# A hybrid decoder block on one core: attention's turns dealt out by the kind of dense output, and a fourth place for split rows

## The chip, the cores and the metric

The kernel runs on one core of a Trainium2 chip. The metric is device time in microseconds for one execution, taken as the median over several runs; less is better. One more execution was recorded by the hardware profiler, and all views in this text come from that one.

## The reference

One layer of a decoder block on x, a sequence of 2048 rows of 1024 numbers, all in float32:

- hn = RMSNorm(x); [u | q | k | v] = hn @ w_in, where each of the four parts is 512 wide.
- Pool mixer: u is cut into four groups of 128 columns. Each group takes a causal running mean over a window (2, 4, 8 and 16 rows), subtracts the row itself, multiplies by a 128 x 128 matrix and by a scale.
- Stick-breaking attention with 8 heads of 64: z = q k / 8, and row t gives to an earlier row s the weight sigmoid(z_ts) times the product of (1 - sigmoid(z_tj)) over all j between s and t. The weights multiply v.
- h = x + concat[RMSNorm(pool), RMSNorm(attention)] @ w_out
- y = RMSNorm(h + relu(RMSNorm(h) @ w_up)^2 @ w_down), with a hidden width of 4096.

## The kernel before, in words

The sequence is cut into four tiles of 512 rows (tile 0 to 3). All rows lie transposed: 128 features across the partitions, 512 rows along the free side. To keep float32 accuracy each operand is split into a high and a low part (`split`, lines 145 and 146: ScalarE copies the high part, VectorE subtracts it from the source), and each product is made of three matmuls, high x high, high x low and low x high.

The front half of the program, which the change touches, computes the input projection and attention. The projection of one tile is cut into 16 **dense outputs** of 128 columns (c = 0 to 3 are the four pool groups, 4 to 7 q, 8 to 11 k, 12 to 15 v). One dense output is 24 matmuls of 512 columns (lines 177 to 179, `products`) into one of two PSUM places (`pd`). What follows depends on the kind. For q and k ScalarE and VectorE split the result (`keep_qk`, tile `qk`) and four DMAs store it. For v ScalarE copies it, TensorE transposes it, and a split of the transposed rows is stored (`keep_v`, tile `vt`). For a pool group (`pool_group`) ScalarE copies it to `u`, VectorE makes c + 1 running sums `s` (line 400), the difference `pl` (line 403) and a split (`pls`, ScalarE the high part, VectorE the low one); then come three matmuls of 512 columns (`pp`, lines 410 to 412: the first and the third need the high part, the second the low one), and ScalarE scales the result to `yb`. So a pool output asks much more of VectorE than the others, most of all c = 3, whose window is 16. The splits `qk`, `vt`, `pls` and `mix` (the normed mixer outputs) share a ring of three places in SBUF, tag `st`.

Attention goes by **turns**. A turn is one head of one tile and one half of its 512 rows (`near_unit`): four matmuls for the logits `pz` (lines 630 and 631), two sigmoids `sh` and `sg` on ScalarE, a mask on GpSimd (line 661), a product scan `pc` on VectorE (line 663), a multiply `sg` (line 672, or 668 for the first rows), and in the next turns four transposes `pta` (line 677) with a split `at`, and six matmuls `po` (line 689) with `v`. Every second turn ends a head with a copy and an add (`ot`, lines 647 and 648). Each head's q, k and v are loaded again by SyncE's queue (lines 623 to 625 and 714 to 717). There are 16 turns to a tile, 64 in all, and they stand in one queue (`todo`), filled by `attend` when their q, k and v are there.

How many turns go with a dense output is set by `state["ratio"]`: half-way through a dense output and after it, `advance` adds half the ratio to an account, and takes turns from the queue while the account is above zero; each turn costs 0.27 (`yield 0.27` in `near`). A ratio of 0.4 so gives about one and a half turns to a dense output. `front(q)` writes the order for the tiles a = 2q and b = 2q + 1: first a's outputs of heads 0 to 3 and the pool groups, then a block in which a and b share the weights of heads 4 to 7, then b's pool groups and heads 0 to 3 (for q = 1 in the other order, pool last). It sets the ratio three times for each q:

```python
RATIO_FRONT = (0.3, 0.4, 0.15, 0.4, 0.4, 0.3)
```

Beside this, `later` holds pieces of the norms (squares, sums and normed chunks `nt`, `h`, `mix`), one or two of which go with each dense output. The program is written in this order, and a scheduler then sets the order of the instructions on each engine, within what the data and the marks of the program allow; a turn may so stand later, though not earlier, than the matmul behind which it was written.

The program before, in what the change touches:

Of the kernel before, what the change touches and what calls it, by code (L numbers as in the profile page):

```python
# [9 lines left out]
F32R = mybir.dt.float32r  # L10
# [5 lines left out]
P = 128  # L16
S = 2048
D = 1024
T = 512
# [3 lines left out]
DH = 64  # L23
# [4 lines left out]
TB = T // P  # L28
# [2 lines left out]
WINDOWS = (2, 4, 8, 16)  # L31
PAD = 15
EPS = 1e-6
RATIO_FRONT = (0.3, 0.4, 0.15, 0.4, 0.4, 0.3)
RATIO_TAIL = 0.6
SR = 3
LB = 4
# [4 lines left out]
POOL, EARLY, FIRST = (0, 1, 2, 3), (4, 8, 12, 5, 9, 13), (4, 8, 5, 9, 12, 13)  # L42
# [3 lines left out]
def hymba_block(ctx: ExitStack, tc: tile.TileContext, xT, gains, w_in, pool_w, w_out, w_up, w_down, out):  # L46
# [239 lines left out]
        return (hpb if j % 2 else hpa).tile([P, 2, T], F32R, tag="h", name="h", align_bytes=256)  # L286

    def make_st():
        return pa.tile([P, 2, T], F32R, tag="st", name="mix", align_bytes=256, bufs=3)


    pw = []
# [14 lines left out]
    def note(emit):  # L307
        prog.append((0, emit, False))

    todo, begun, finished, state = [], {}, set(), {"gran": 0, "tick": 0, "due": 0.0}  # L310


    st = [{} for _ in range(NT)]
# [71 lines left out]
    def pool_group(j, g, ps):  # L385
        w = WINDOWS[g]
        if g == 0:
            st[j]["y"] = pa.tile([P, 4, T], F32, tag="yb", name="yb", bufs=1)
        u = pa.tile([P, PAD + T], F32, tag="u", name="u")
        nc.gpsimd.tensor_copy(u[:, 0:PAD], carry[:, g])  # L390
        if j == 0:
            took = nc.vector.tensor_tensor(u[:, PAD:], ps, st[0]["r"], ALU.mult)
        else:
            took = nc.scalar.activation(u[:, PAD:], ps, AF.Copy)
        nc.gpsimd.tensor_copy(carry[:, g], u[:, T:T + PAD])
        cur, lag = u, 1
        while lag < w:
            nxt = pa.tile([P, PAD + T], F32, tag="s", name="s")
            lo = 2 * lag - 1
            nc.vector.tensor_tensor(nxt[:, lo:], cur[:, lo:], cur[:, lo - lag:PAD + T - lag], ALU.add)  # L400
            cur, lag = nxt, 2 * lag
        pl = pa.tile([P, T], F32, tag="ev", name="pl")
        nc.vector.scalar_tensor_tensor(pl, cur[:, PAD:], 1.0 / w, u[:, PAD:], op0=ALU.mult, op1=ALU.subtract)
        if j == 0:
            nc.vector.tensor_tensor(pl[:, 0:w - 1], cur[:, PAD:PAD + w - 1], recip[:, 0:w - 1], ALU.mult)
            nc.vector.tensor_tensor(pl[:, 0:w - 1], pl[:, 0:w - 1], u[:, PAD:PAD + w - 1], ALU.subtract)
        d = pa.tile([P, 2, T], F32R, tag="st", name="pls", align_bytes=256, bufs=3)
        split((d[:, 0], d[:, 1]), pl)
        pp = psx.tile([P, T], F32, tag="px", name="pp")
        nc.tensor.matmul(pp, pw[0][:, 0, g], d[:, 0], start=True, stop=False)  # L410
        nc.tensor.matmul(pp, pw[0][:, 0, g], d[:, 1], start=False, stop=False)
        nc.tensor.matmul(pp, pw[0][:, 1, g], d[:, 0], start=False, stop=True)
        nc.scalar.activation(st[j]["y"][:, g], pp, AF.Copy, scale=gs[:, g:g + 1])
        return took
# [16 lines left out]
        normed(4, part, g, make_st, lambda: st[j]["rm"], mx[j][at:at + 4])  # L431

    def keep_qk(j, c, dst, ps):
        d = pa.tile([P, 2, T], F32R, tag="st", name="qk", align_bytes=256, bufs=3)
        if j == 0:
            t = pa.tile([P, T], F32, tag="ev", name="qkr")
            nc.vector.tensor_tensor(t, ps, st[0]["r"], ALU.mult)
            ps = t
        took = split((d[:, 0], d[:, 1]), ps)
        for e in range(2):  # L440
            for x in range(2):
                nc.sync.dma_start(dst[2 * c + e][j][x * DH:(x + 1) * DH].bitcast(F32),
                                  d[e * DH:(e + 1) * DH, x].bitcast(F32))
        return took

    def keep_v(j, c, ps):
        vf = pa.tile([P, T], F32, tag="ev", name="vf")
        if j == 0:
            took = nc.vector.tensor_tensor(vf, ps, st[0]["r"], ALU.mult)
        else:  # L450
            took = nc.scalar.activation(vf, ps, AF.Copy)
        pt = psx.tile([P, TB, 2, DH], F32, tag="px", name="ptv")
        for b in range(TB):
            nc.tensor.transpose(pt[:, b], vf[:, b * P:(b + 1) * P], ident)
        vt = pa.tile([P, 2, TB, 2, DH], F32R, tag="st", name="vt", align_bytes=256, bufs=3)
        split((vt[:, :, :, 0], vt[:, :, :, 1]), pt.rearrange("p b e d -> p e b d"))
        for e in range(2):
            nc.sync.dma_start(vs[2 * c + e][j].bitcast(F32),
                              vt[:, e].rearrange("p b x d -> p (b x d)").bitcast(F32))
        return took  # L460
# [47 lines left out]
    def front(q):  # L508


        a, b = 2 * q, 2 * q + 1

        def rate(i):
            note(lambda: state.update(ratio=RATIO_FRONT[3 * q + i]))
        rate(0)
        if q == 0:
            note(start)
            note(norm1_first)
            note(pool_weights)
        else:  # L520
            note(lambda: (load_x(b, bigp), norm1_rms(b), norm1(b), pace(2)))
        for i, c in enumerate((EARLY if q else FIRST) + POOL):
            if q == 0 and i == 2:
                note(lambda: load_x(b, x0p))
            if q == 0 and i == 4:
                note(lambda: (norm1_rms(b), catch_up(len(later)), norm1(b)))
            if q == 0 and i == 8:
                note(lambda: (catch_up(len(later)), to_att(), load_x(b + 1, bigp)))
                attend(a, 0)
                attend(a, 1)  # L530
            in_proj(a, c)
            if q and i in (2, 5):
                attend(a, i // 3)
        note(lambda: (catch_up(len(later)), pool_norm(a)))
        rate(1)
        for h2 in (2, 3):
            note(lambda h2=h2: (norm1_rms(2) if h2 == 2 else None) if q == 0 else attn_norm(0) if h2 == 2 else None)
            for c in range(4 + h2, 16, 4):
                in_proj(a, c)
                in_proj(b, c, True)  # L540
            attend(a, h2)
            attend(b, h2)
        note(lambda: (catch_up(len(later)), (load_acc(0), load_mix(0, KD), attn_norm(1)) if q else norm1(b + 1), pace(1)))
        rate(2)
        for i, c in enumerate(EARLY + POOL if q else POOL + EARLY):
            if q == 0 and i == 4:
                note(lambda: pool_norm(b))
            if q == 0 and i == 6:
                note(lambda: pace(2))
            if q and i == len(EARLY):  # L550
                note(lambda: (catch_up(len(later)), pace(1)))
            in_proj(b, c)
            if i in ((2, 5) if q else (6, 9)):
                attend(b, i // 3 % 2 if q else i // 9)
        note(lambda: (catch_up(len(later)), (pool_norm(b), catch_up(len(later))) if q else None))
# [1109 lines left out]
```

## Time and profile before

| what | value |
|---|---|
| median of 3 runs | 1903.73 us (1903.68 to 1907.18) |
| the profiled execution's own time | 1902.05 us |
| its span, first to last instruction | 1900.3 us |
| TensorE matmuls, busy | 1868.9 us (98%), 8883 instructions |
| VectorE, busy | 1481.2 us (78%) |
| ScalarE, busy | 1025.2 us (54%) |
| GpSimd, busy | 238.5 us (13%) |
| mean granted TensorE clock | 0.995 |

The span leaves out some 1.8 us that lie around it. PE is TensorE's matmuls, DVE VectorE, ACT ScalarE, POOL GpSimd, SPq the queue of SyncE. In rows of the timeline the first number is the start in us from the span's start, the second the duration in us; the bracket at the end is the engine's idle time before the row and what ended it. Matmuls overlap, so the time from one start to the next counts, not the duration. In a table of windows PEclk is the clock that was granted, as a share of full speed.

### The profile page before, as it was taken

The numbers are of one execution on the slowest core, as the hardware profiler recorded it, in microseconds if no ns is written. First come the engines' busy times: TensorE is split into PE (matmuls) and PEld (weight loads), VectorE is DVE, ScalarE is ACT, GpSimd is POOL, SyncE is SP. The second block draws the span as 40 slices with busy tenths as digits, with TensorE's granted clock in tenths as the row PEclk, the third lists the DMA queues.
The fourth block names the chain that finished last, engine by engine and source line by source line (L and its number), as shares of the span: only waits on it lengthen the run. The fifth ranks groups of instructions, "written<-read, shape, count | busy, mean of one in ns | idle before, by whom it ended". The sixth has DMA issues, their size and how long they took to land.

```text
span 1900.3 us, 26640 instructions
## 1 busy us (share of the span) xinstructions
PE 1868.9 (98%) x8883; PEld 1554.3 (82%) x8883; DVE 1481.2 (78%) x2151; ACT 1025.2 (54%) x1616; POOL 238.5 (13%) x463
## 2 busy tenths in 40 slices
PE   9999999999999999999999999999999999999997
PEld 7788788788888888777888888887888888888886
DVE  6887789678866886778799988786666677988774
ACT  6565567455644465554567555554332665656543
POOL 0233234122321050000000000000010010020120
PEclk9999999999999999999999999999999999999998
DMA  7676596699888777787899888889999899999852
GB/s 226 212 255 201 177 313 224 194 322 315 281 310 312 278 252 254 284 303 274 307 358 328 303 308 281 298 284 333 388 313 330 281 317 307 332 294 341 289 206 91
DMA packets 222164, 535.91 MB, mean 282 GB/s; under 512 B 26048, under 2 KB 32192, under 8 KB 218176
## 3 DMA queue, kind: packets, MB, share of 16 engines
q1 hardware_dynamic: 217264, 525.46, 79.4%
q0 software_dynamic: 4608, 8.39, 2.4%
q8 instruction: 72, 1.18, 0.3%
q14 instruction: 76, 0.62, 0.1%
q10 hardware_dynamic: 144, 0.26, 0.0%
HBM read 349.46 MB, written 184.55 MB: 281 GB/s over the span
## 4 chain that ended last, share of the span: by engine, by line
PE 50%; DMA 5%; DVE 2%; issue 1%; ACT 1%; POOL 0%; SPq 0%; DVEq 0%; ACTq 0%
PE pb L1291 14%; PE pY L1118 13%; PE pb L1468 12%; PE pZ L1118 7%; PE pX L1118 3%; DMA ar<-sd 1%; DMA hn<-hs 1%; DMA ar<-sdi 1%; PE pb L1408 1%; DMA td<-t 0%; DMA t<-in_w_down_dram 0%; DMA b<-in_w_down_dram 0%; DMA wr<-in_w_down_dram 0%; DVE ad L146 0%; DVE hw L146 0%
## 5 line engine op out<-in xcount | busy, mean ns | idle before, releaser
L1118 PE MATMUL pY<-sa,hw 128*128 128x512 f32 x1536 | 366.3, 390 | 1.9 <-ACT u L1041 1.9
L1118 PEld LDWEIGHTS pY<-sa,hw 128*128 128x128 f32 x1536 | 287.9, 188 | 63.0 <-ACT u L1041 3.4
L1291 PE MATMUL pb<-ad,wd 128*128 128x512 f32 x1344 | 305.4, 389 | 0.7 <-DVE ad L146 0.7
L177 PE MATMUL pd<-h,hl 128*128 128x512 f32 x752 | 297.9, 396 | 1.5 <-DVE qk L146 1.3
L178 PE MATMUL pd<-h,hl 128*128 128x512 f32 x752 | 297.0, 395 | 0.3 <-DVE h L146 0.3
L179 PE MATMUL pd<-h,hl 128*128 128x512 f32 x752 | 297.3, 395 | 0.0
L1291 PEld LDWEIGHTS pb<-ad,wd 128*128 128x128 f32 x1344 | 252.1, 188 | 53.8 <-DVE ad L146 1.5
L1468 PE MATMUL pb<-ad,wd 128*128 128x512 f32 x1104 | 253.9, 390 | 0.9 <-ACT ad L145 0.9
L1468 PEld LDWEIGHTS pb<-ad,wd 128*128 128x128 f32 x1104 | 206.5, 188 | 44.6 <-ACT ad L145 1.3
L146 DVE TENSOR_TENSOR ad<-ar,ad 128x1024 fp32r<-128x1024 f32 x160 | 194.1, 1221 | 44.1 <-ACT ad L145 43.5
L145 ACT ACTIVATE ad<-ar 128x1024 fp32r<-128x1024 f32 x160 | 168.4, 1054 | 95.7 <-PE pb L1468 31.9
L1118 PE MATMUL pZ<-sa,hw 128*128 128x512 f32 x768 | 186.8, 390 | 1.7 <-DVE a L1061 1.7
L1118 PEld LDWEIGHTS pZ<-sa,hw 128*128 128x128 f32 x768 | 143.9, 188 | 32.7 <-DVE a L1061 3.0
L145 ACT ACTIVATE hl<-raw 128x512 fp32r<-128x512 f32 x168 | 104.1, 629 | 115.6 <-PE pd L179 76.7
L177 PEld LDWEIGHTS pd<-h,hl 128*128 128x128 f32 x752 | 142.2, 189 | 29.0 <-DVE qk L146 1.8
L179 PEld LDWEIGHTS pd<-h,hl 128*128 128x128 f32 x752 | 142.0, 189 | 28.2 <-DVE hl L146 0.5
L178 PEld LDWEIGHTS pd<-h,hl 128*128 128x128 f32 x752 | 142.2, 189 | 27.1 <-DVE h L146 0.7
L146 DVE TENSOR_TENSOR hl<-raw,hl 128x512 fp32r<-128x512 f32 x168 | 115.1, 690 | 46.9 <-ACT hl L145 46.5
L1035 ACT ACTIVATE a<-a 128x512 f32<-128x512 f32 x96 | 60.1, 629 | 89.6 <-DVE a L1077 38.5
L146 DVE TENSOR_TENSOR hw<-rt,hw 128x512 fp32r<-128x512 f32 x128 | 86.5, 686 | 25.2 <-ACT hw L145 25.1
L145 ACT ACTIVATE wd<-wq 128x1024 fp32r<-128x1024 f32 x56 | 59.4, 1060 | 77.1 <-PE pb L1291 68.4
L146 DVE TENSOR_TENSOR wd<-wq,wd 128x1024 fp32r<-128x1024 f32 x56 | 68.5, 1222 | 34.3 <-ACT wd L145 32.8
(218 smaller groups left out, 2737.3 us busy)
## 6 DMA issues: line engine op xcount, KB each, us to landing
ar<-sd SPq DMA_DIRECT2D x96, 512.0 KB, 5.9
ar<-sdi SPq DMA_DIRECT2D x64, 512.0 KB, 5.6
rb<-in_w_up_dram SPq DMA_DIRECT2D x30, 1024.0 KB, 6.2
sd<-a SPq DMA_DIRECT2D x104, 256.0 KB, 5.2
raw<-in_w_in_dram SPq DMA_DIRECT2D x50, 512.0 KB, 4.6
sdi<-hr SPq DMA_DIRECT2D x96, 256.0 KB, 5.4
wr<-in_w_down_dram SPq DMA_DIRECT2D x48, 512.0 KB, 5.7
sd<-s SPq DMA_DIRECT2D x88, 256.0 KB, 4.9
```

The source lines that it names most:

```text
L145: nc.scalar.activation(hi, src, AF.Copy)
L146: return nc.vector.tensor_tensor(lo, src, hi.bitcast(F32), ALU.subtract)
L177: nc.tensor.matmul(ps, hl[:, 0, c], hi, start=(k == 0), stop=False)
L178: nc.tensor.matmul(ps, hl[:, 0, c], lo, start=False, stop=False)
L179: last_mm[0] = nc.tensor.matmul(ps, hl[:, 1, c], hi, start=False, stop=(k == n - 1))
L1035: nc.scalar.activation(t, src, AF.Relu)
L1118: nc.tensor.matmul(t, w[:, wx, c], a[:, ax, c % 2], start=first and c == 0 and x == 0, stop=last and c == G - 1 and x == 2, skip_group_che ...
L1291: nc.tensor.matmul(b, t[:, wx, 2 * (kk % 2) + c, i * P:(i + 1) * P], a[:, ax, c], start=p in ("P1", "P5", "P2") and kk == 0 and c == 0 and ...
L1408: nc.tensor.matmul(b[:, cols], block(t, wx, c, n), a[:, ax, c, cols], start=False, stop=(i == 1 and c == 1 and x == 2), skip_group_check=True)
L1468: nc.tensor.matmul(ps[q, n], block(t, wx, c, n), left_[q][:, ax, c], start=(n_ in ("P1", "P3") and kk == 0 and c == 0 and x == 0), stop=(n ...
```

## The change

The ratio now depends on q, on the stage and, in the first and third stage, on whether the output is a pool group. The second number of a pair is that of the pool outputs:

```diff
-RATIO_FRONT = (0.3, 0.4, 0.15, 0.4, 0.4, 0.3)
+PACE = (((0.3, 0.3), 0.4, (0.25, 0.1)), ((0.25, 0.1), 0.4, (0.4, 0.25)))
...
-        return pa.tile([P, 2, T], F32R, tag="st", name="mix", align_bytes=256, bufs=3)
+        return pa.tile([P, 2, T], F32R, tag="st", name="mix", align_bytes=256, bufs=4)
...
-        def rate(i):
-            note(lambda: state.update(ratio=RATIO_FRONT[3 * q + i]))
-        rate(0)
+        def rate(r):
+            note(lambda: state.update(ratio=r))
...
         for i, c in enumerate((EARLY if q else FIRST) + POOL):
+            rate(PACE[q][0][c in POOL])
...
-        rate(1)
+        rate(PACE[q][1])
...
-        rate(2)
         for i, c in enumerate(EARLY + POOL if q else POOL + EARLY):
+            rate(PACE[q][2][c in POOL])
```

The tiles `pls`, `qk` and `vt` get `bufs=4` in the same way as `mix`. So the first stage of q = 0 (tile 0) and both shared blocks keep their ratios. Tile 1's pool outputs go from 0.15 to 0.1 and its other outputs from 0.15 to 0.25; tile 2's from 0.4 to 0.25, its pool outputs to 0.1; tile 3's from 0.3 to 0.4, its pool outputs to 0.25. What a turn computes, and the order of the turns among themselves, stay as they were.

Where the turns go is seen in the order of the instructions. On VectorE, the last pool output of tile 2 (c = 3) before the change: its sums `s` lead to `pl_4176`, `pc`, `sg`, `at` and `ot` are of turns, `ss` is of a norm, `hl` are weights. Ahead of these rows, behind the first sum `s_4168<-u_4164`, stand one more multiply `sg`, one more scan `pc` and one `ss`.

```order
L648 TENSOR_TENSOR ot_4127<-ot_4127,po_4029 64x512
L400 TENSOR_TENSOR s_4170<-s_4168 128x524
L146 TENSOR_TENSOR pls_4082<-pl_4080,pls_4082 128x512
L672 TENSOR_TENSOR sg_4288<-sg_4288,pc_4281 128x2x255
L146 TENSOR_TENSOR at_4214<-pta_4209,at_4214 128x512
L400 TENSOR_TENSOR s_4172<-s_4170 128x520
L146 TENSOR_TENSOR hl_4416<-raw_4106,hl_4416 128x512
L663 SCALAR_TENSOR_TENSOR pc_4347<-sh_4352,later_keys_106 128x512
L400 TENSOR_TENSOR s_4174<-s_4172 128x512
L672 TENSOR_TENSOR sg_4354<-sg_4354,pc_4347 128x2x255
L146 TENSOR_TENSOR at_4277<-pta_4272,at_4277 128x512
L403 SCALAR_TENSOR_TENSOR pl_4176<-s_4174,u_4164 128x512
```

The same place after the change, from the first sum on; `pl_3971` is the same difference.

```order
L400 TENSOR_TENSOR s_3963<-u_3959 128x526
L146 TENSOR_TENSOR at_3998<-pta_3993,at_3998 128x512
L663 SCALAR_TENSOR_TENSOR pc_4002<-sh_4007,later_keys_106 128x512
L400 TENSOR_TENSOR s_3965<-s_3963 128x524
L146 TENSOR_TENSOR pls_3908<-pl_3906,pls_3908 128x512
L189 TENSOR_TENSOR ss_4055<-ss_4055,sq_4057 128x512
L672 TENSOR_TENSOR sg_4009<-sg_4009,pc_4002 128x2x255
L400 TENSOR_TENSOR s_3967<-s_3965 128x520
L400 TENSOR_TENSOR s_3969<-s_3967 128x512
L403 SCALAR_TENSOR_TENSOR pl_3971<-s_3969,u_3959 128x512
```

Between the first sum and `pl` stood 14 rows with two scans; now stand 8 rows with one, and over all four pool outputs of the tile three scans are left of seven.

On TensorE, the three pool matmuls `pp` of that output before the change stand behind the `po` matmuls of two turns, at the end of a dense output (`pd_4424` is the next).

```order
L689 MATMUL po_4331<-at_4277,vw_4197 64x128
L689 MATMUL po_4331<-at_4343,vw_4197 128x256
L689 MATMUL po_4331<-at_4343,vw_4197 128x128
L689 MATMUL po_4331<-at_4343,vw_4197 64x128
L689 MATMUL po_4331<-at_4343,vw_4197 64x256
L689 MATMUL po_4331<-at_4343,vw_4197 128x128
L689 MATMUL po_4331<-at_4343,vw_4197 64x128
L410 MATMUL pp_4181<-pls_4178,pw_656 128x512
L411 MATMUL pp_4181<-pls_4178,pw_656 128x512
L412 MATMUL pp_4181<-pls_4178,pw_656 128x512
L177 MATMUL pd_4424<-h_2455,hl_4103 128x512
```

After the change the same three (`pp_3976`) stand among the last matmuls of the dense output `pd_4091`.

```order
L178 MATMUL pd_4091<-h_3983,hl_3926 128x512
L410 MATMUL pp_3976<-pls_3973,pw_656 128x512
L179 MATMUL pd_4091<-h_3983,hl_3926 128x512
L677 MATMUL pta_4111<-ident_98,sg_4085 128x128 x4
L630 MATMUL pz_4200<-kw_4136,qa_4131 128x256
L411 MATMUL pp_3976<-pls_3973,pw_656 128x512
L412 MATMUL pp_3976<-pls_3973,pw_656 128x512
```

The matmuls of the turns around them have gone to the dense outputs behind; the place itself, about two dense outputs behind the one that they belong to, is the same.

On VectorE, the last pool output of tile 1 before the change, the end of its chain to the split `pls_2649`:

```order
L663 SCALAR_TENSOR_TENSOR pc_2777<-sh_2782,later_keys_106 128x512
L648 TENSOR_TENSOR ot_2766<-ot_2766,po_2662 64x512
L400 TENSOR_TENSOR s_2645<-s_2643 128x512
L672 TENSOR_TENSOR sg_2784<-sg_2784,pc_2777 128x2x255
L740 TENSOR_SCALAR zero_2912<-left0_137 128x16
L146 TENSOR_TENSOR at_2773<-pta_2769,at_2773 128x384
L146 TENSOR_TENSOR hl_2822<-raw_2745,hl_2822 128x512
L403 SCALAR_TENSOR_TENSOR pl_2647<-s_2645,u_2635 128x512
L741 TENSOR_REDUCE zall_141<-zero_2912 128x1
L146 TENSOR_TENSOR pls_2649<-pl_2647,pls_2649 128x512
```

And after the change, the same end:

```order
L400 TENSOR_TENSOR s_2645<-s_2643 128x512
L146 TENSOR_TENSOR hl_2822<-raw_2745,hl_2822 128x512
L663 SCALAR_TENSOR_TENSOR pc_2806<-sh_2811,later_keys_106 128x512
L403 SCALAR_TENSOR_TENSOR pl_2647<-s_2645,u_2635 128x512
L648 TENSOR_TENSOR ot_2795<-ot_2795,po_2712 64x512
L672 TENSOR_TENSOR sg_2813<-sg_2813,pc_2806 128x2x255
L146 TENSOR_TENSOR at_2802<-pta_2798,at_2802 128x384
L740 TENSOR_SCALAR zero_2891<-left0_137 128x16
L146 TENSOR_TENSOR pls_2649<-pl_2647,pls_2649 128x512
```

Here the scan of the third turn stands still ahead of `pl`; `ot`, `sg` and `at` have moved from ahead of it to between `pl` and `pls`.

More of the change, by code (lines that the diff above doesn't have):

```diff
@@ L406, in pool_group @@
             nc.vector.tensor_tensor(pl[:, 0:w - 1], pl[:, 0:w - 1], u[:, PAD:PAD + w - 1], ALU.subtract)
-        d = pa.tile([P, 2, T], F32R, tag="st", name="pls", align_bytes=256, bufs=3)
+        d = pa.tile([P, 2, T], F32R, tag="st", name="pls", align_bytes=256, bufs=4)
         split((d[:, 0], d[:, 1]), pl)
@@ L433, in keep_qk @@
     def keep_qk(j, c, dst, ps):
-        d = pa.tile([P, 2, T], F32R, tag="st", name="qk", align_bytes=256, bufs=3)
+        d = pa.tile([P, 2, T], F32R, tag="st", name="qk", align_bytes=256, bufs=4)
         if j == 0:
@@ L454, in keep_v @@
             nc.tensor.transpose(pt[:, b], vf[:, b * P:(b + 1) * P], ident)
-        vt = pa.tile([P, 2, TB, 2, DH], F32R, tag="st", name="vt", align_bytes=256, bufs=3)
+        vt = pa.tile([P, 2, TB, 2, DH], F32R, tag="st", name="vt", align_bytes=256, bufs=4)
         split((vt[:, :, :, 0], vt[:, :, :, 1]), pt.rearrange("p b e d -> p e b d"))
```

## The prediction

> **What bounds the kernel now.** I read the page first. TensorE is busy nearly the whole span:
>
> ```profile
> span 1900.3 us, 26640 instructions
> PE 1868.9 (98%) x8883; PEld 1554.3 (82%) x8883; DVE 1481.2 (78%) x2151; ACT 1025.2 (54%) x1616; POOL 238.5 (13%) x463
> ```
>
> The change removes no matmul, so all it can win is what is missing there: gaps on TensorE and stretches in which its clock is not granted in full. Then I looked for those in the front half, with a table of windows:
>
> ```profile
> 200.00:210.00 10.00, 6.36 (x38) 5.11 (x36) 9.62 (x19) 4.24 (x8) 4.84 (x3) 1.00 0.69 224
> 210.00:220.00 10.00, 9.43 (x34) 7.43 (x35) 5.79 (x10) 5.37 (x11) 0.00 (x0) 0.83 0.61 150
> 330.00:340.00 10.00, 7.83 (x48) 6.26 (x47) 10.00 (x16) 6.12 (x11) 6.46 (x4) 1.00 0.25 87
> 340.00:350.00 10.00, 9.34 (x38) 7.73 (x39) 8.29 (x13) 4.97 (x9) 0.79 (x3) 0.66 0.65 176
> ```
>
> Columns behind the length: PE, PEld, DVE, ACT and POOL busy, then PEclk. At two places TensorE loses time while VectorE (third) is full, 9.62 and 10.00 of 10 us, and after each the clock is down, to 0.83 and 0.66. The timeline of TensorE shows what waits there:
>
> ```profile
> 210.35 0.50 PE L410 MATMUL pp<-pls,pw 128*128 128x512 f32 x1 [3.98 <-ACT pls L145]
> 211.07 0.79 PE L411 MATMUL pp<-pls,pw 128*128 128x512 f32 x1 [0.22 <-DVE pls L146]
> ...
> 212.09 0.63 PE L177 MATMUL pd<-h,hl 128*128 128x512 f32 x1
> 212.52 0.63 PE L178 MATMUL pd<-h,hl 128*128 128x512 f32 x1
> ...
> 334.54 0.49 PE L411 MATMUL pp<-pls,pw 128*128 128x512 f32 x1 [0.30 <-DVE pls L146]
> ...
> 339.87 0.66 PE L677 MATMUL pta<-ident,sg 128*128 128x128 f32 x4 [1.87 <-DVE at L146]
> 341.19 2.18 PE L689 MATMUL po<-at,vw 128*128 128x256 f32 x12 [0.67 <-DVE ot L648]
> ```
>
> Both stand in the last pool outputs of a tile: stall 1 (tile 1) waits for `pls`, stall 2 (tile 2) for the splits of the turns that pile up there. Stall 1 costs 3.98 + 0.22 = 4.2 us of gaps and (1 - 0.83) x 10 = 1.7 us of clock, 5.9 in all. Stall 2 costs 0.30 + 1.87 + 0.67 = 2.84 us of gaps and (1 - 0.66) x 10 = 3.4 us of clock, 6.2 in all. No other gap behind 112 us in the front reaches 1 us.
>
> **Tile 2, where turns are taken out.** VectorE's rows of the three marks of that place, the first sum of c = 0, the first sum of c = 3 and its `pl`:
>
> ```profile
> 298.89 0.70 DVE L400 TENSOR_TENSOR s<-u 128x526 f32<-128x526 f32 x1
> ...
> 329.66 0.69 DVE L400 TENSOR_TENSOR s<-u 128x526 f32<-128x526 f32 x1
> ...
> 339.74 0.67 DVE L403 SCALAR_TENSOR_TENSOR pl<-s,u 128x512 f32<-128x512 f32 x1
> ```
>
> The prices of single steps come from the same engine at stall 1, from one start to the next, where it ran without a gap; the last rows give the way from `pl` to TensorE, with ScalarE's row between:
>
> ```profile
> 184.47 0.71 DVE L400 TENSOR_TENSOR s<-u 128x526 f32<-128x526 f32 x1 [0.21 <-ACT u L394]
> ...
> 204.72 1.22 DVE L663 TENSOR_TENSOR_SCAN pc<-sh,later_keys 128x512 f32<-128x512 f32 x1
> 205.86 0.65 DVE L648 TENSOR_TENSOR ot<-ot,po 64x512 f32<-64x512 f32 x1
> 206.44 0.67 DVE L400 TENSOR_TENSOR s<-s 128x512 f32<-128x512 f32 x1
> 207.04 0.67 DVE L672 TENSOR_TENSOR sg<-sg,pc 128x510 f32<-128x510 f32 x1
> ...
> 207.88 0.55 DVE L146 TENSOR_TENSOR at<-pta,at 128x384 fp32r<-128x384 f32 x1
> 208.35 0.68 DVE L146 TENSOR_TENSOR hl<-raw,hl 128x512 fp32r<-128x512 f32 x1
> 208.95 0.68 DVE L403 SCALAR_TENSOR_TENSOR pl<-s,u 128x512 f32<-128x512 f32 x1
> ...
> 210.33 0.69 DVE L146 TENSOR_TENSOR pls<-pl,pls 128x512 fp32r<-128x512 f32 x1 [0.62 <-ACT pls L145]
> ```
>
> ```profile
> 209.66 0.63 ACT L145 ACTIVATE pls<-pl 128x512 fp32r<-128x512 f32 x1 [2.63 <-DVE pl L403]
> ```
>
> So a scan takes 205.86 - 204.72 = 1.14 us, a step of 512 columns 207.04 - 206.44 = 0.60, one of 384 columns 0.47, `ot` 0.58. From the start of `pl` to that of the first `pp` go 210.35 - 208.95 = 1.4 us, and the second `pp` follows 211.07 - 210.33 = 0.74 behind the start of VectorE's `pls`. The method can be tested: before the change 14 rows, two of them scans, stand between the sum at 329.66 and `pl`. That makes 13 x 0.60 + 2 x 1.14 = 10.1 us, and the trace has 339.74 - 329.66 = 10.08.
>
> After the change 8 rows with one scan stand there: 8 x 0.60 + 1.14 = 5.9 us. VectorE was also late when it came to that sum: from the first sum of c = 0 it took 329.66 - 298.89 = 30.8 us. In the new order the way between the same marks holds 31 steps, one of them a scan and five of them `nt` (0.67, an estimate from its busy time), which makes 20.3 us. TensorE needs 18.5 us for its own work between the two outputs (an estimate from matmuls at the spacings below). So VectorE comes to that sum 1.8 us late, and `pl` starts some 0.75 + 1.8 + 5.9 = 8.5 us behind the end of the dense output (0.75 is an estimate for ScalarE's copy `u` of 0.6 us and the hand-over), `pp` could start 1.4 us later, at 9.9 us. TensorE's own way to that place, by its order, is 53 matmuls of 512 columns and 32 small ones, at these spacings:
>
> ```profile
> 242.21 0.39 PE L178 MATMUL pd<-h,hl 128*128 128x512 f32 x1
> 242.44 0.39 PE L179 MATMUL pd<-h,hl 128*128 128x512 f32 x1
> 242.66 0.65 PE L689 MATMUL po<-at,vw 128*128 128x256 f32 x6
> 243.14 0.62 PE L677 MATMUL pta<-ident,sg 128*128 128x128 f32 x4
> ```
>
> 53 x 0.227 + 32 x 0.1 = 15.2 us (242.66 - 242.44 gives 0.22; 0.48 / 6 = 0.08 for a `po`, and 0.1 taken as a mean). There are 5 us in hand, so stall 2 goes: -6.2 us. If VectorE came 5 us later than summed, the stall would come back.
>
> **Tile 1, where the order keeps the turns.** The ratio there falls from 0.15 to 0.1, but the order on VectorE, which was never idle from 184.47 (the sum of c = 2) to `pl`, holds in between one scan more (1.14) for one `at` (0.47), one `ot` (0.58) and the small `zero` (0.1, an estimate) less; the other steps are the same. That is a difference of 0.0 us, and `pl` starts where it did, at about 208.95. Behind it `ot`, `sg`, `at` and `zero` now come ahead of `pls`, 0.58 + 0.60 + 0.47 + 0.1 = 1.75 us, so the low half is ready at 208.95 + 0.6 + 1.75 + 0.74 = 212.0 and not at 211.07. TensorE comes to the place with the same matmuls behind it. Stall 1 stays, and grows by 0 to 1 us, nearer to the upper end, as `pls` is a fixed count of steps behind `pl`: I take +0.8. Bounds for the place as a whole: 2 us less if `pl` comes early, 2 us more if the scan ahead of it waits, as its logits now stand just six rows ahead of `pp` on TensorE.
>
> **Where the turns go.** By the ratios 11 turns went with the 12 outputs that tiles 2 and 3 share, and 17 will; tile 3's pool outputs get 4 for 5. That stage stands here (and the wait that is nearest to its danger, TensorE waiting for a PSUM place until VectorE has split `qk`):
>
> ```profile
> 357.00:425.00 68.00, 68.00 (x389) 58.52 (x388) 46.40 (x66) 37.15 (x69) 14.54 (x42) 1.00 0.87 293
> ```
>
> ```profile
> PE pd L177 <- DVE qk L146: 1.3, 2, 0.8
> ```
>
> A turn costs VectorE 1.14 + 0.60 + 0.60 + 0.58 / 2 = 2.6 us; six are 16 us, and this window has 21.6 us idle. The turn brings its 14 matmuls along (some 1.4 us at 0.1), so the window also grows, by the 8 us that tile 2's own stage loses: no change in the sum. GpSimd (mask and a small copy) has 13% to do, and the loads of a head go on SyncE's queue in the same order with the same turns; no row of TensorE is released by a DMA. I cost it at nothing, within 1 us to either side. If the cover is gone, a dense output waits as at those two rows: 0.8 us each without the clock, some 6 with it.
>
> **The ring of four.** It takes away waits on ScalarE:
>
> ```profile
> ACT mix L145 <- DMA vs<-vt: 5.9, 2, 3.7
> ...
> ACT mix L145 <- DMA mx<-mix: 2.9, 1, 2.9
> ```
>
> These 8.8 us are hidden, since ScalarE is busy 54% and TensorE had no gap at those places. I cost it at nothing (0 to -1 us).
>
> **A rule on the clock.** After stall 1 matmuls start 212.52 - 212.09 = 0.43 us apart, about twice 0.227, and after stall 2, whose longest gap is 1.87 us, the window has 0.66. The Trainium skill, "TensorE: Matmul & The Clock Gate", section "What's actually happening", says that the clock goes to half after an idle window of about 3.4 us. The half agrees with the rows; for the gap of stall 2 the trace does not, since 1.87 and 0.67 us were enough. By the rule alone the slow stretch there would have another cause and could remain, and the sum would be less; I go by the rows.
>
> **Sum.** -6.2 + 0.8 = -5.4 us. The profiled execution took 1902.05 us, so 1896.7; the median of the runs stands 1.7 us above it, and on it the forecast is 1898.3. What can be told from no change in this kernel is about 0.2%, 3.8 us.
>
> **The rivals.**
> - Both stalls go: VectorE's `pl` in tile 1 comes over 3.4 us sooner than summed, for instance because ring waits had held it. For it: ScalarE's idle of 2.63 us ahead of `pls`. Against it: that wait ended with VectorE's `pl`. -6.2 - 5.9 = -12.1, 1891.6. Chance 0.08.
> - The slow stretch of stall 2 stays though its gaps go, as other gaps under 2 us bring it about: -2.84 + 0.8 = -2.0, 1901.7. Chance 0.08.
> - One new stall of the size of stall 2 in the stage that now has 17 turns: -5.4 + 6.2 = +0.8, 1904.5, no change. Chance 0.15. For it: the wait at `qk`; against it: 21.6 us of idle time.
> - Slower: VectorE falls behind twice in that shared stage, so that the split of `qk` comes later than the 5.4 us (24 x 0.227) that the other PSUM place covers, each time with the slow clock behind it: -5.4 + 2 x 6.2 = +7.0, 1910.7. It decides from two turns' work (5.2 us) piled up at one dense output. Chance 0.12.
> - That the change does not do what it says holds for tile 1, and is in the sum; for tile 2 the order shows that it does.
>
> **How the numbers follow.** The forecast, stall 2 gone and stall 1 left, has 0.57, and its own range is 1894.5 to 1901 (2 us less or more for stall 1, 1 us each for the shared stage and the ring); 0.04 of it lie within 3.8 us of 1903.7. Faster is 0.53 + 0.08 = 0.61, no change 0.04 + 0.08 + 0.15 = 0.27, slower 0.12. The range leaves out the first and the fourth rival (0.20): 1894 to 1905.
>
> **What would show it.** Right: no gap over 0.5 us at `pp` of tile 2 and PEclk 1.00 there; the gap at `pp` of tile 1 still near 4 us with the clock down behind it; no gap over 1 us in the shared stage of tiles 2 and 3. Wrong: the gap of tile 1 under 1 us, or a new row of TensorE that waits over 1 us for `qk`, `at` or `pls` and a window behind it with a clock under 0.9.

## The result, and the profile after

The changed kernel is slower: 1915.58 us (median of 5 runs, 1912.4 to 1917.46) against 1905.84 us of the kernel before in the same set; the ratio is 1.0062, with a 95% interval of 1.0046 to 1.0077. The forecast was 1898.3, faster. The profiled execution took 1916.48 us, 14.4 us more than that of the kernel before, where the medians are 9.7 us apart; what is counted below is counted in the two profiled ones. The head of its page:

```profile
span 1914.8 us, 26666 instructions
...
PE 1871.9 (98%) x8883; PEld 1558.2 (81%) x8883; DVE 1484.2 (78%) x2151; ACT 1027.1 (54%) x1616; POOL 233.8 (12%) x463
```

The span is 14.5 us longer, and the shares of the engines are what they were: they say nothing. The same table of windows as in the prediction (length; PE, PEld, DVE, ACT and POOL busy; PEclk; DMA share; GB/s):

```profile
200.00:210.00 10.00, 6.06 (x34) 4.66 (x32) 9.97 (x18) 5.94 (x11) 2.86 (x4) 0.99 0.54 185
210.00:220.00 10.00, 9.45 (x33) 7.64 (x34) 5.60 (x10) 3.06 (x6) 0.00 (x0) 0.67 0.57 152
250.00:260.00 10.00, 6.70 (x38) 5.43 (x36) 5.15 (x9) 5.01 (x10) 0.00 (x0) 1.00 0.99 336
260.00:270.00 10.00, 8.38 (x32) 7.00 (x33) 7.39 (x12) 5.04 (x10) 1.26 (x2) 0.66 0.64 201
310.00:360.00 50.00, 50.00 (x281) 42.59 (x281) 44.23 (x69) 29.53 (x54) 20.02 (x33) 1.00 0.72 226
...
357.00:425.00 68.00, 68.00 (x409) 59.10 (x408) 54.79 (x77) 42.87 (x79) 16.31 (x39) 1.00 0.89 293
...
550.00:560.00 10.00, 6.04 (x34) 4.98 (x33) 3.57 (x6) 2.72 (x6) 0.00 (x0) 0.89 1.03 407
560.00:570.00 10.00, 6.29 (x19) 5.33 (x20) 6.90 (x11) 6.13 (x11) 3.50 (x8) 0.50 1.03 393
```

Stall 2 is gone (310 to 360: PE 50.00 of 50, clock 1.00). Stall 1 is there. Two stretches are new, around 260 and around 560 us, and in both VectorE and ScalarE are far from full (2.7 to 7.4 us of 10 busy): this is not an engine that has too much to do. What TensorE waits for there, in its timeline:

```profile
208.86 0.50 PE L410 MATMUL pp<-pls,pw 128*128 128x512 f32 x1 [3.31 <-ACT pls L145]
...
210.55 0.80 PE L411 MATMUL pp<-pls,pw 128*128 128x512 f32 x1 [1.19 <-DVE pls L146]
...
261.62 0.80 PE L177 MATMUL pd<-h,hl 128*128 128x512 f32 x1 [4.92 <-DVE qk L146]
...
563.71 1.86 PE L205 MATMUL pm<-inv,ss 128*128 128x1 f32 x8 [7.67 <-DVE ss L189]
```

The third is **stall 3**: a dense output of tile 2, just behind the end of tile 1, finds no PSUM place, since `qk` has not been split. The last is **stall 4**: in the output projection, which follows the front, the mean `pm` for the norm of tile 2's attention output waits for the sum of squares `ss`. Counted as gap + (1 - clock) x busy time of the windows behind it, stall 1 costs 4.50 + 0.33 x 9.45 = 7.6 us (5.8 before, counted so), stall 3 costs 4.92 + 0.34 x 8.38 = 7.8 (a gap of 0.76 before), stall 4 costs 7.67 + 0.11 x 6.04 + 0.50 x 6.29 = 11.5, and stall 2 nothing (6.0 before). That makes 1.8 + 7.0 + 11.5 - 6.0 = 14.3 of the 14.5 us. That it comes so near is in part chance: TensorE's first matmul of the hidden layers (line 1118), behind all four places, starts 11.5 us later than before (700.7 against 689.2 us), so the count is some 3 us too high, and another 3 us are lost behind that point, where TensorE waits 4.4 us for `a` in place of 1.7.

**How stall 3 comes about.** ScalarE's timeline at that place, and further down the row behind which stall 4 begins:

```profile
248.03 1.66 ACT L145 ACTIVATE mix<-nt 128x512 fp32r<-128x512 f32 x3
...
257.90 0.63 ACT L145 ACTIVATE mix<-nt 128x512 fp32r<-128x512 f32 x1 [4.17 <-DMA vs<-vt]
258.44 0.58 ACT L145 ACTIVATE at<-pta 128x512 fp32r<-128x512 f32 x1
258.92 0.59 ACT L636 ACTIVATE sh<-pz 128x512 f32<-128x512 f32 x1
259.39 0.60 ACT L638 ACTIVATE sg<-pz 128x512 f32<-128x512 f32 x1
259.87 0.61 ACT L145 ACTIVATE qk<-pd 128x512 fp32r<-128x512 f32 x1
...
559.89 0.63 ACT L185 ACTIVATE ss<-ol 128x512 f32<-128x512 f32 x1 [2.58 <-DMA ol<-os]
```

`vt` and three `mix` fill the ring of four. The fourth `mix` needs the place of `vt`, and gets it only when the store `vs<-vt` has landed. ScalarE works in order, so the split of `qk` stands behind that wait, with three rows between, and TensorE behind the split.

**How stall 4 comes about.** SyncE's queue (a row's second number is the time over which its DMAs were issued; `mx` and `os` are where the rows `mix` and the attention output lie in the chip's main memory, and `h<-mx` loads the former again for the output projection):

```profile
250.13 0.85 SPq L458 DMA_DIRECT2D vs<-vt  x2
...
543.78 1.44 SPq L561 DMA_DIRECT2D h<-mx  x2
...
545.86 0.99 SPq L561 DMA_DIRECT2D h<-mx  x2
546.94 0.39 SPq L280 DMA_DIRECT2D mx<-mix  x1
...
553.73 0.33 SPq L159 DMA_DIRECT2D raw<-in_w_out_dram  x1
554.99 0.88 SPq L810 DMA_DIRECT2D ol<-os  x2
```

The load `ol` (tile 2's attention output) waits for the store of tile 3's last `mix`: the program makes it wait for that store, in every kernel here. The store, issued at 546.94, takes 8.0 us to land, and `ol` is issued at 554.99. Before, SyncE's rows, then ScalarE's at the two hand-overs, then TensorE's:

```profile
245.75 0.32 SPq L458 DMA_DIRECT2D vs<-vt  x1
...
540.22 0.32 SPq L280 DMA_DIRECT2D mx<-mix  x1
...
544.88 0.88 SPq L810 DMA_DIRECT2D ol<-os  x2
```

```profile
251.33 0.63 ACT L145 ACTIVATE mix<-nt 128x512 fp32r<-128x512 f32 x1 [2.25 <-DMA vs<-vt]
...
549.98 0.64 ACT L185 ACTIVATE ss<-ol 128x512 f32<-128x512 f32 x1 [0.32 <-DMA ol<-os]
```

```profile
256.07 0.50 PE L177 MATMUL pd<-h,hl 128*128 128x512 f32 x1 [0.76 <-DVE qk L146]
...
555.37 0.95 PE L205 MATMUL pm<-inv,ss 128*128 128x1 f32 x8
```

So both waits stood in the kernel before, and were all but covered: from the start of `ss` to `pm` the chain takes 563.71 - 559.89 = 3.8 us where TensorE waits for it, and before it had 555.37 - 549.98 = 5.4 us. There were 1.6 us in hand. Two things used them up. The order brought the store nearer to `pm`: from its issue to the moment at which `pm` wants to start (its start less its wait, 563.71 - 7.67 = 556.04) there are 556.04 - 546.94 = 9.1 us, before 555.37 - 540.22 = 15.2 us, so 6.1 us less. And the store took 8.0 us to land in place of 4.7, 3.3 us more. Together 9.4 us, less the 1.6 in hand, make 7.8; the wait is 7.67.

### The profile page after: what moved, and what is told of

Its sections match the earlier page's. It is cut to its first block, busy times and chain, and to the rows that moved or that the text cites. A ratio compares the mean times of both kernels' runs of the same rounds, so it can differ in the third digit from the quotient of the medians.

```text
span 1914.8 us, 26666 instructions
## 1 busy us (share of the span) xinstructions
PE 1871.9 (98%) x8883; PEld 1558.2 (81%) x8883; DVE 1484.2 (78%) x2151; ACT 1027.1 (54%) x1616; POOL 233.8 (12%) x463
## 4 chain that ended last, share of the span: by engine, by line
PE 51%; DMA 3%; DVE 2%; issue 1%; ACT 1%; POOL 0%; SPq 0%; DVEq 0%; ACTq 0%
PE pb L1291 16%; PE pY L1118 13%; PE pb L1468 12%; PE pZ L1118 7%; PE pX L1118 3%; DMA hn<-hs 1%; DMA ar<-sd 1%; PE pb L1408 1%; DMA td<-t 0%; DMA t<-in_w_down_dram 0%; DMA b<-in_w_down_dram 0%; DVE hw L146 0%; DVE a L1077 0%; DMA su<-hs 0%; DVE a L1073 0%
```

## The experiments

Ratios are to the kernel before, run on the same chip in the same set (its medians, one for each set: 1901.96, 1903.75, 1903.4 and 1902.43 us). The table sums the runs up: how tile 1, 2 and 3 get their turns ("old" as before, "new" as changed), the places of the ring, and the two waits of TensorE in us, with any other single wait of 2 us or more that the kernel before does not have.

| run | tiles 1, 2, 3 | places | stall 3 | stall 4 | other | ratio, 95% interval |
|---|---|---|---|---|---|---|
| before | old, old, old | 3 | 0.8 | 0 | | 1 |
| after | new, new, new | 4 | 4.9 | 7.7 | | 1.0062 (1.0046 to 1.0077) |
| e1_pace_ring3 | new, new, new | 3 | 5.8 | 0 | `pr` for `yrlast` 4.0 | 1.0035 (1.0023 to 1.0048) |
| e2_ring_only | old, old, old | 4 | 0 | 1.7 | | 1.0014 (1.0001 to 1.0027) |
| e3_tile3_old | new, new, old | 4 | 3.9 | 4.4 | `pY` for `u` 2.2 | 1.0044 (1.003 to 1.0058) |
| e4_tile2_ring3 | old, new, old | 3 | 1.7 | 2.2 | | 1.0011 (1.0001 to 1.002) |
| f1_tile1_old | old, new, new | 4 | 0.5 | 0 | | 0.9957 (0.9944 to 0.9969) |
| f2_tile1_old_ring3 | old, new, new | 3 | 0.9 | 0 | `pY` for `u` 2.0 | 0.9986 (0.997 to 1.0002) |
| g1_vs_on_act | as after | 4 | 3.1 | 8.5 | | 1.0035 (1.0023 to 1.0046) |
| g2_ol_on_act | as after | 4 | 2.7 | 14.3 | `pY` for `u` 2.2, `pd` for `acc` 2.1 | 1.0071 (1.0048 to 1.0093) |
| h1_pool_01 | (0.15, 0.1), new, new | 4 | 1.9 | 0 | | 0.9983 (0.997 to 0.9996) |
| h2_qkv_025 | (0.25, 0.15), new, new | 4 | 0 | 1.6 | | 0.9989 (0.9974 to 1.0004) |
| k3_root_later | as after | 4 | 3.1 | 5.5 | | 1.0043 (1.0029 to 1.0057) |
| e5_tile2_ring4 | old, new, old | 4 | 0 | 0 | `pr` for `yrlast` 4.4 | 0.9988 (0.9976 to 1.0) |
| k4_root_earlier | as after | 4 | 3.1 | 11.7 | | 1.0064 (1.0046 to 1.0083) |

**First four: the ring or the dealing?** The parts of the change, taken apart:

```diff
e1_pace_ring3:   bufs=4 -> bufs=3 in the four tiles of the ring, PACE as changed
e2_ring_only:    RATIO_FRONT as before, bufs=4
e3_tile3_old:    PACE's last pair (0.4, 0.25) -> (0.3, 0.3)
e4_tile2_ring3:  tile 1 (0.15, 0.15), tile 2 (0.25, 0.1), tile 3 (0.3, 0.3), bufs=3
```

> The turns dealt out as in the changed kernel, the ring for split rows left at three places. Theory R (the ring is the fault: with four places the scheduler sets a mix whose place only the slow store of vt gives back ahead of work that TensorE needs): the wait of pd for qk at tile 2's first outputs, 4.92 us in the changed kernel, is under 1.5 us; the wait of pm for ss in the tail, 7.67 us, is under 2 us; stall 2 stays away and stall 1 stays; time 3 to 6 us under the kernel before. Theory T (the dealing of the turns is the fault, the ring does nothing): both new waits stand as in the changed kernel, time 8 to 12 us over the kernel before.

> The turns as in the kernel before, the ring with four places. Theory R: stall 2 stays (a loss of about 6 us as before), the wait of pd for qk at tile 2's first outputs is 4 to 5 us, and there may be a wait of 5 us or more of pm for ss; time 6 to 15 us over the kernel before. Theory T: no new wait over 1.5 us, time within 2 us of the kernel before.

> The changed kernel with tile 3's turns at the old ratio, the ring with four places. Theory R: both new waits stand (4 to 5 us of pd for qk at tile 2's first outputs, 5 us or more of pm for ss), time within 3 us of the changed kernel. Theory T, in the form that tile 3's dealing makes the later wait: the wait of pm for ss is under 2 us and the time is 9 to 13 us under the changed kernel's, the wait of pd for qk stands.

> Only tile 2's turns are dealt out anew, tiles 1 and 3 at the old ratios, three places. Theory R: stall 2 gone, stall 1 as before (about 4 us of gap), no new wait over 1.5 us, time 5 to 7 us under the kernel before. Theory T, in the form that tile 2's dealing is the fault: the wait of pd for qk at tile 2's first outputs is 4 to 5 us, time within 3 us of the kernel before.

Theory R fell at once. With three places stall 3 is there all the same (5.75 us), with four places and the old turns it is not. TensorE's timeline of e1_pace_ring3, with a third wait, that for a root that GpSimd works out, and SyncE's rows for stall 4:

```profile
262.24 0.80 PE L177 MATMUL pd<-h,hl 128*128 128x512 f32 x1 [5.75 <-DVE qk L146]
...
709.58 1.61 PE L231 MATMUL pr<-identr,yrlast 128*128 128x128 f32 x6 [3.97 <-POOL yrlast L834]
```

```profile
539.96 0.53 SPq L280 DMA_DIRECT2D mx<-mix  x1
...
544.20 0.88 SPq L810 DMA_DIRECT2D ol<-os  x2
```

Stall 3 so goes with the dealing. Stall 4 does not stand here, so theory T, which wanted both, fell too. With four places it does, in three sizes in this group (1.7, 4.4 and 7.7 us), but e4_tile2_ring3 has one of 2.2 us with three places: the ring alone does not make it. e3_tile3_old, with tile 3's old turns, kept both waits, stall 4 at 4.4 us, which is neither the 5 us or more of theory R nor the under 2 us of theory T. Stall 2 is gone wherever tile 2 has the new turns, and stands where it has not (e2_ring_only: `pta` for `at` 1.9 us). Neither theory foresaw e4_tile2_ring3: stall 2 gone, and the time still 0.1% over the kernel before; part of what was won at stall 2 shows as longer waits at other hand-overs (2.2 us for `ss`, 1.7 for `qk`, 1.3 more than before for `u` in the hidden layers); where the rest went was not found.

**Next four: one cause or two, and what holds the store and the load up.**

```diff
f1_tile1_old:        PACE's first new pair (0.25, 0.1) -> (0.15, 0.15), bufs=4
f2_tile1_old_ring3:  the same, bufs=3
g1_vs_on_act:        -nc.sync.dma_start(vs[2 * c + e][j]...
                     +(nc.scalar if j == 1 and c == 1 else nc.sync).dma_start(vs[2 * c + e][j]...
g2_ol_on_act:        -nc.sync.dma_start(ol[i], ...
                     +(nc.scalar if j == 2 else nc.sync).dma_start(ol[i], ...
```

> The changed kernel with tile 1's turns at the old ratios (0.15 for all its outputs); tiles 2 and 3 dealt out anew, four places. Theory D (each new wait has its own cause: the earlier one tile 1's dealing whatever the ring, the later one the ring of four, made longer by tile 3's dealing): pd's wait for qk at tile 2's first outputs is under 2 us, stall 1 is back at 4.0 us, the wait of pm for ss stays at 5 us or more; time 5 to 9 us under the changed kernel. Theory C (one cause: the delay made at tile 1 is carried on and brings the later wait): both waits under 2 us, time at or under the kernel before.

> As the run with tile 1's old ratios, with three places. Theory D: stall 2 gone, stall 1 at 4.0 us, neither new wait (each under 2 us); what is left over 1.5 us is small, time 3 to 6 us under the kernel before. Theory S (whatever is dealt out anew, the static order puts some other hand-over too late, as it did in the tail of two runs so far): a new wait of 1.5 us or more somewhere behind 400 us, time within 3 us of the kernel before or over it.

> The changed kernel; the two stores of vt of tile 1's last v output are issued by ScalarE in place of SyncE, on its own DMA queue; the order is otherwise the same, row for row. Theory Q (the store is late because it stands behind a dozen loads of q, k and v on SyncE's queue): it lands 2 to 3 us sooner, the fourth mix waits under 2 us (4.2 now), pd's wait for qk falls from 4.92 to 1 to 3 us and its slow clock with it, time 3 to 7 us under the changed kernel. Theory B (the DMA engines are full, whoever issues): it lands as late, the wait stays over 4 us, time within 3 us of the changed kernel.

> The changed kernel; the two loads ol of tile 2's attention output are issued by ScalarE in place of SyncE, so that they don't stand behind raw there. Theory D (the wait of pm for ss comes from these loads standing behind two weight loads in SyncE's queue): ol is issued before 550 us, the wait of pm for ss (7.67 us) falls under 3 us, time 5 to 10 us under the changed kernel. Rival (pm has been put too early on TensorE's order, and the load only looks late because all of it is): the wait stays over 5 us, time within 3 us of the changed kernel.

f1_tile1_old is the run that tells most: one pair of numbers taken back, and both new stalls are gone. Theory C had that right, theory D, which wanted stall 4 to stay, did not. The time is 1896.16 us against 1903.75, and this is a version that beats both kernels. TensorE's timeline, three windows of the table, and SyncE's rows for stall 4:

```profile
208.72 0.50 PE L410 MATMUL pp<-pls,pw 128*128 128x512 f32 x1 [3.98 <-ACT pls L145]
...
253.31 0.50 PE L177 MATMUL pd<-h,hl 128*128 128x512 f32 x1 [0.52 <-DVE qk L146]
```

```profile
250.00:260.00 10.00, 9.48 (x52) 7.93 (x52) 8.73 (x14) 7.79 (x15) 3.74 (x2) 1.00 0.76 238
...
310.00:360.00 50.00, 50.00 (x294) 43.15 (x293) 43.22 (x64) 31.30 (x58) 16.23 (x33) 1.00 0.86 278
...
550.00:560.00 10.00, 10.00 (x53) 8.54 (x52) 3.79 (x7) 3.16 (x6) 6.61 (x25) 1.00 0.85 298
```

```profile
530.49 0.32 SPq L280 DMA_DIRECT2D mx<-mix  x1
...
533.63 1.43 SPq L810 DMA_DIRECT2D ol<-os  x2
```

f2_tile1_old_ring3 has neither stall, and still comes out near no change, as theory S said: its largest new wait is one of 2.0 us for `u` in the hidden layers.

g1_vs_on_act is inconclusive. Its order is the changed kernel's, but for the two stores. Here are ScalarE's row and TensorE's of it, and then ScalarE's and TensorE's of k3_root_later (below), which leaves this place alone:

```profile
255.41 0.63 ACT L145 ACTIVATE mix<-nt 128x512 fp32r<-128x512 f32 x1 [1.84 <-DMA vs<-vt]
```

```profile
259.13 0.79 PE L177 MATMUL pd<-h,hl 128*128 128x512 f32 x1 [3.06 <-DVE qk L146]
```

```profile
255.54 0.63 ACT L145 ACTIVATE mix<-nt 128x512 fp32r<-128x512 f32 x1 [2.30 <-DMA vs<-vt]
```

```profile
259.26 0.50 PE L177 MATMUL pd<-h,hl 128*128 128x512 f32 x1 [3.06 <-DVE qk L146]
...
564.22 1.86 PE L205 MATMUL pm<-inv,ss 128*128 128x1 f32 x8 [5.51 <-DVE ss L189]
```

The wait of 3.06 us is at the edge of what theory Q expected (1 to 3 us), but a kernel that leaves the stores with SyncE has the same. From issue to the `mix` that waits for it the store took 7.8 us in the changed kernel, 5.2 in e3_tile3_old, 6.2 in g2_ol_on_act, 6.3 in k3_root_later, 6.4 in k4_root_earlier, and 5.5 when ScalarE issued it: no better than the spread. The Trainium skill, "DMA: Bandwidth & Descriptors", section "Issuing engines are not separate DMA queues", says that DMAs of all engines end up on the same 16 DMA engines, and that another issuer saves issue time alone; this run agrees.

The spread serves for something else. In these six kernels, which share the order at this place, the row of TensorE starts 3.72 or 3.73 us behind the start of that `mix`, whether the `mix` came at 253.92 or at 257.90. So it is this wait that TensorE waits out, in each of them.

g2_ol_on_act missed, and no theory had it: the wait grew to 14.3 us. ScalarE issued the loads at 550.98, still 9.2 us behind the store of the last `mix`, and waited for the second of them until 562.93. Why they are so late was seen in the last run.

**Last five.**

```diff
h1_pool_01:       tile 1 (0.15, 0.1)
h2_qkv_025:       tile 1 (0.25, 0.15)
k3_root_later:    -if c == (2 if j == 0 else 4) and j + 2 < NT:
                  +if c == (3 if j == 0 else 4) and j + 2 < NT:
e5_tile2_ring4:   tile 1 (0.15, 0.15), tile 2 (0.25, 0.1), tile 3 (0.3, 0.3), bufs=4
k4_root_earlier:  +if c == (1 if j == 0 else 4) and j + 2 < NT:
```

> The changed kernel with tile 1's q, k and v outputs at the old 0.15 and its pool outputs at the new 0.1. Theory Q (the earlier new wait comes from the 0.25, which puts turns of tile 1, and the loads of their heads, ahead of the last store of vt): pd's wait for qk at tile 2's first outputs is under 2 us, time 4 to 9 us under the changed kernel. Rival P (the 0.1 is the fault: the turns kept out of the pool outputs come later, beside the pool norm): the wait is 4 us or more.

> The changed kernel with tile 1's q, k and v outputs at the new 0.25 and its pool outputs at the old 0.15. Theory Q: pd's wait for qk is 4 to 6 us, time within 4 us of the changed kernel. Rival P: the wait is under 2 us, time 4 to 9 us under the changed kernel.

Neither number alone makes stall 3 (1.9 and 0 us). Rival P fell by the first run, theory Q, which laid it on the 0.25, by the second: it takes both. What the seven kernels with both have in common is the lead of the store. From its issue to the moment at which TensorE wants to start (its start less its wait) there are 5.0 to 7.2 us (the changed kernel 256.70 - 250.13 = 6.6); where the other kernels show it, 8.5 to 9.6 (before 255.31 - 245.75 = 9.6, f1_tile1_old 252.79 - 244.23 = 8.6, h1_pool_01 8.6). In these kernels the store takes 5 to 8 us and the way from `mix` to TensorE 3 to 5, so under some 9 us TensorE waits. But the lead is not all. SyncE's row and TensorE's of h2_qkv_025:

```profile
248.49 0.79 SPq L458 DMA_DIRECT2D vs<-vt  x2
```

```profile
255.84 0.39 PE L177 MATMUL pd<-h,hl 128*128 128x512 f32 x1
```

Its store has a lead of 7.4 us, about that of the seven, and the same row of TensorE did not wait, since the two stores landed in 2.3 and 2.6 us. By the landing times in the traces, one earlier load of SyncE's was still under way when they were issued, in the changed kernel six. (The count alone does not tell it: in h1_pool_01 there were three, and the store took 6.8 us.) So stall 3 takes a store that is both late and slow; what makes it slow was not tried alone. h2_qkv_025 has no wait for `pls` at stall 1's place either (its longest gap there is 1.2 us), and yet it is only 0.1% under the kernel before: TensorE starts its hidden layers 3.3 us earlier (685.9 against 689.2 us), and the profiled span ends 1.9 us later. What it loses behind that point was not followed up.

> The changed kernel; the root of tile 2's attention norm is taken up one output later (at the fourth output of the projection of tile 0 in place of the third). The loads ol keep their place on SyncE, behind the same rows; pm, which waits for them through ss, stands 21 rows of 0.227 us, 4.8 us, later on TensorE. Theory L (the later new wait is the lead that the order leaves between these loads and pm, as the loads come late): the wait of pm for ss falls by 4.8 us, from 7.67 to 2 to 4 us, and the loss there from 11.9 to 3 to 6 us; time 5 to 9 us under the changed kernel. Rival (loads and pm move together, since VectorE, not the load, is late): the wait stays over 6 us.

Half of it: the wait fell by 2.2 us, not by 4.8, to 5.5, as the store took 9.1 us to land and not 8.0, and from the landing of the second load to `pm` went 4.1 us and not 2.2. The ratio is 0.2% under the changed kernel's, with intervals that overlap, where 5 to 9 us had been expected.

> Only tile 2's turns dealt out anew, four places. If tile 3's dealing does nothing of its own: like the run with tile 1's old ratios, 6 to 9 us under the kernel before. If it is needed to keep ol early: a wait of pm for ss of 2 us or more, as in the run of tile 2 alone with three places, and a time within 3 us of the kernel before.

Between the two: no wait for `ss`, but one of 4.4 us for `yrlast`, 0.12% under the kernel before. TensorE came to the hidden layers 9.2 us earlier than before (680.0 against 689.2 us), the most of all runs, but the profiled span is only 3.4 us shorter.

> The changed kernel; the root of tile 2's attention norm is taken up one output earlier (at the second output of the projection of tile 0 in place of the third). On SyncE the loads ol stand ahead of the second weight load raw, not behind it; on TensorE pm stands 24 rows of 0.227 us, 5.4 us, earlier. Theory L (ol is late because it stands behind that raw, which waits until a weight tile is used up): ol is issued 5 to 8 us earlier against the front's progress, so within 3 us of the last store mx, and as pm stands 5.4 us earlier too, the wait of pm for ss stays at 5 to 8 us and the time within 4 us of the changed kernel. Rival V (ol waits for something of its own, the end of tile 2's attention or the place in SBUF): it is issued no earlier than 3 us before the time in the changed kernel, and the wait of pm for ss grows to 10 us or more.

Rival V was right in the wait, 11.7 us, and the weight load was not the cause. (`ol` was issued 4.6 us earlier than in the changed kernel, more than the 3 us that V allowed, but so was the store, by 4.7.) `raw` now stood behind `ol`, and `ol` was still issued 8.1 us behind the store of the last `mix`. SyncE's rows and TensorE's:

```profile
542.26 0.45 SPq L280 DMA_DIRECT2D mx<-mix  x1
...
550.35 0.91 SPq L810 DMA_DIRECT2D ol<-os  x2
```

```profile
559.00 1.87 PE L205 MATMUL pm<-inv,ss 128*128 128x1 f32 x8 [11.71 <-DVE ss L189]
```

The traces show two parts. One is the time that the store took to land: 8.0 us here and in the changed kernel, 9.1 in k3_root_later, 8.4 in g1_vs_on_act, 8.3 in g2_ol_on_act, 5.6 in e3_tile3_old, and 2.7 to 6.4 in the nine other kernels (4.7 before, 4.2 in e1_pace_ring3, 2.7 in f1_tile1_old, 6.4 in e2_ring_only, 6.1 in h2_qkv_025); in all fifteen `ol` was issued within a microsecond of that landing. In the five slow ones three or four loads `h<-mx` of 512 KB were issued in the 3.3 us ahead of the store, in e3_tile3_old one, in the nine others none. (That these loads make the store slow is read from the traces together; no run took them away alone.) The other part is the lead from the store's issue to the moment at which `pm` wants to start: 547.29 - 542.26 = 5.0 us here, 9.1 in the changed kernel, and 15.2 to 16.0 in the six kernels without stall 4.

## Why the prediction was wrong

- **Stall 2 goes, -6.2 us: right.** In the changed kernel and in every run with tile 2's new turns there is no gap over 0.3 us at that place, and the clock is 1.00. The working held too: in the changed kernel VectorE took 20.8 us from the first sum of c = 0 to that of c = 3, and 6.2 us from there to `pl`, where 20.3 and 5.9 had been summed.
- **Tile 1, +0.8 us, bounds -2 to +2: right in kind, its size in part luck.** The gap shrank to 3.31 us and the second one grew from 0.22 to 1.19, 0.3 us together; the +1.8 us come from a clock of 0.67 instead of 0.83, and e1_pace_ring3 and g2_ol_on_act, with the same two gaps, had 0.83 and 0.84 there. VectorE took 24.4 us from the sum of c = 2 to `pl`, as forecast (24.5 before), but began 1.5 us earlier, which the forecast did not have.
- **Where the turns go: this step failed.** "I cost it at nothing, within 1 us to either side." For the stage of tiles 2 and 3, where it looked, it held: TensorE was busy 68.00 of 68 us while VectorE went from 46.40 to 54.79. But it looked at that stage alone. Tile 1's turns go too, from the pool outputs to the q, k and v outputs behind them: in TensorE's order all four turns of tile 1's heads 6 and 7 (24 turns in all) now stand ahead of tile 2's first output, where two of the four stood before. There the store of `vt` has 3.0 us less lead (6.6 for 9.6) and waits for its landing 2.2 us longer (7.8 for 5.6), and stall 3 arose, +7.0 us. With tile 1's pair taken back (f1_tile1_old) the ratio falls by 1.05%, 20 us: that is what this step left out.
- **"No row of TensorE is released by a DMA": true, and no ground.** A store does not release TensorE; it gives a place back to a row of ScalarE or to a load, behind which TensorE's row stands. The two rows that the prediction quoted, `mix` waiting for `vs<-vt` and for `mx<-mix`, were called hidden since ScalarE is busy 54%. ScalarE's mean says nothing here: the first of the two had TensorE waiting 0.76 us behind it before the change.
- **The ring of four, 0 to -1 us: not one number.** With the old turns it costs 0.14% (0.01 to 0.27), with tile 1 old and the others new it is worth 3.7 us (1896.16 against 1899.89), with all new it brings stall 4, +11.5 us by the count above, but only 0.27% (1.0062 against 1.0035), 5 us, between the ratios, as e1_pace_ring3 loses at `yrlast` instead.
- **The rivals.** That of the slower side had two new stalls and a sum of +7.0 us over the kernel before, where the medians stand 9.7 apart; its place and mechanism were wrong. VectorE did not fall behind in the shared stage: one new stall lies 95 us ahead of that stage and the larger one some 130 us behind it, in a stage that the change does not name.
- **Without tile 1's pair the forecast holds**: f1_tile1_old has stall 2 gone, stall 1 as it was, and is 0.43% (0.31 to 0.56) faster, 5.9 to 10.7 us on 1903.75, where the sum without its term for tile 1 says 6.2.

Open is why the order for the pair, and with four places only, puts four loads ahead of the last `mix` store, some 290 us behind tile 1's last outputs. The order comes from a scheduler that works through the whole program, and these runs show which orders it made, not why. It wasn't tried to hold the order fixed while a ratio changes.

## What to carry to other kernels

An order that was tuned by hand or by a scheduler can leave little in hand at a hand-over (here 1.6 us at one and nothing at another), so a table that sets the order is to be priced over all that follows it, and not only in the stages that it names. Look, at each place where instructions move, for rows that wait for a store: a ring's place is only free when the store has landed, and what stands behind the waiting row in its engine's queue waits too, however idle that engine is on average. When a change of several numbers loses, take them back one group at a time before it is given up: here all of the loss, and a gain behind it, hung on one pair.

## What the runs showed of the hardware that was not expected

- The time of one store of the same size goes with what was issued just before: 512 KB landed in 2.7 to 6.4 us with no load `h<-mx` in the 3.3 us before (nine kernels), in 8.0 to 9.1 us with three or four such loads of 512 KB (five kernels).
- TensorE's clock after a gap: in h1_pool_01 a single gap of 1.88 us at 253.49 left it at 1.00, in k3_root_later one of 3.06 brought the next 10 us to 0.84, in the changed kernel one of 4.92 to 0.66. The same gaps do not give the same clock either: behind stall 2, with 1.87 and 0.67 us close together, it was 0.66 before and 0.83 in e2_ring_only; behind 3.31 and 1.19 us it was 0.67 in the changed kernel and 0.84 in g2_ol_on_act. So a price for the clock that is read from one profile can be off by half.
- GpSimd's steps on 128x4 numbers are not of one length. In the chain ahead of the wait for `yrlast` in e1_pace_ring3 two steps of one line took 1.06 and 0.20 us (GpSimd's timeline below); the twelve steps there took from 701.78 to 709.28 us. Seven of the eight steps of 0.5 us or more among them end 0.13 or 0.14 us behind the start of a row of VectorE. In the kernel before, three steps of the chain took 3.4, 4.1 and 5.2 us, and each ended 0.14 us behind the start of VectorE's row `acc<-pd,acc`, which reads PSUM (the longest, and that row, stand below as well). So they seem to wait for VectorE; no run tried it.

```profile
702.98 1.06 POOL L224 TENSOR_TENSOR v<-v 128x4 f32<-128x4 f32 x1
...
709.08 0.20 POOL L224 TENSOR_TENSOR v<-v 128x4 f32<-128x4 f32 x1
```

```profile
677.37 5.17 POOL L222 TENSOR_TENSOR v<-v 128x4 f32<-128x4 f32 x1
```

```profile
682.41 0.68 DVE L827 TENSOR_TENSOR acc<-pd,acc 128x512 f32<-128x512 f32 x1
```
